# Another order of issue for ScalarE, VectorE, GpSimd and SyncE in a decoder-layer kernel with a fixed order of matmuls

## The chip, the core and the metric

The kernel runs on one core of a Trainium2 chip. A core has five engines that are met below under the profile's names: PE (TensorE, the matmuls; PEld is its load of the stationary operand), DVE (VectorE), ACT (ScalarE), POOL (GpSimd) and SP (SyncE, which here only issues DMAs). Each engine runs its own list of instructions strictly in order; engines wait for each other on semaphores. The metric is the device time of one execution in microseconds (us); the median over several executions is compared.

## The reference

One layer of a decoder trunk for a sequence of 256 tokens, model width 1024, all in float32:

```python
h = RMSNorm(x)
u = h @ W_in            # columns: rnn_x | rnn_gate | q | k | v | branch gates ga, gb
A = GeLU(rnn_gate) * RG_LRU(causal_dwconv4(rnn_x))       # recurrent branch
B = MoBA attention(q, k, v), 8 heads of 128, QK-norm     # one block: causal softmax here
y = sigmoid(ga) * (A @ P_A) + sigmoid(gb) * (B @ P_B)
x = x + y @ W_out
h = RMSNorm(x)
x = x + (GeLU(causal_dwconv3(h @ W_up)) * (h @ W_gate)) @ W_down     # D_FF = 2816
```

RG_LRU is `a = exp(-8 r softplus(-lam))`, then `h_t = a_t h_(t-1) + sqrt(1 - a_t^2) i_t x_t` with r and i two sigmoids of block-diagonal products (8 blocks of 128).

## The kernel before

Every product is taken three times on PE: each float32 operand is split into a rounded high part and the rest, and `hi*hi + hi*lo + lo*hi` is summed in PSUM (`mm3`). Most matmuls have 512 columns; those of attention have 128 or 256.

**Weights stream.** All weights pass in pieces of 1 MB: SP issues the load of `raw` (three buffers), ACT casts it to `hi` (four buffers), DVE subtracts to get `lo` (three buffers), and PE uses both. A piece feeds 24 matmuls. The text numbers the pieces: lo25 is the low half of piece 25. The first four pieces (weights of k) are loaded and split in smaller parts, `raws`, `his`, `los`. In the feed-forward part, quarters of the gate's weights (`wq`) are combined on DVE into sums and differences (`wt`, `wq`) for a seven-product scheme, which PE multiplies as qA, qB and qC.

**Stages of PE, in this order:** k, rx and rg (the recurrent branch's inputs), ri (its two gates), q, ga, v, gb with the scores `s` and the outputs `o` of the eight heads in between, pr (A @ P_A), pa (B @ P_B), wo (W_out), then up, gt and q products, `acc` (W_down), with `last` for the eleventh pair of columns of the feed-forward part and `end` for the last quarter of the output.

**Turns.** Where a result must change between token-major and feature-major, it is not transposed on PE but goes out and in again through DRAM: DVE transposes blocks of 32, SP writes the result in four DMAs and reads it back in one (`turn`, `att_t`, `att_r`). The pairs of names are qd and qm (q), kd and km (k), gr and gm (the recurrent branch's gate), xd and xm, pd and pm (a head's probabilities), md and mm (the merged y), fupd and upm, gq and gtm, fld and lastm. A turned q is split into qTh (ACT) and qTl (DVE), probabilities into pth and ptl, the recurrent branch's result into yah and yal, the attention's into ybh and ybl, the merged y into mh and ml, the feed-forward's into fah and fal, with fla for its last pair.

**Small chains.** The reciprocal roots of the norms are found by three Newton steps on 128x8 values: the tile `rsq`, on DVE to start with and, for q and k, on POOL (`rsqrt(..., pool=True)`); the results for k are `rk`, and k is scaled by them (`kr`) before its turn. ACT's functions lie in tables: an ACT_TABLE_LOAD stands in the list wherever the function next asked for isn't in the table that is loaded. The attention's exponentials (`sm`), the sigmoids of the branch gates (`sga`, `sgb`), tanh, sqrt and gelu share ACT with the casts. The greatest score of each row, with the mask added, is found by DVE (`sm`, `mx`), and POOL holds besides the Newton steps the decay's series (`decw`).

**What sets the order.** The body of the program records operations instead of issuing them: the PE ones in a list of their own, all others in one numbered list. At the end `Later.issue` goes through the string `ORDER`: a number n issues recorded operation n on its engine, `a-b` a run of them, and `+n` the next n matmuls. So `ORDER` sets, for each engine, the order of its list, and nothing else decides it; the order among matmuls is that of their recording. `Pool.buffer` gives a tile the buffer whose last use lies furthest back in the same order. All instructions of the trace have line L247, the call in `Later.issue`; they are told apart by tiles. Semaphores come from the true dependencies. A DMA waits also for the DMA that used its semaphore before it, of which there are eight.

Of the kernel before, what the change touches and what calls it, by code (L numbers as in the profile page):

```python
# [115 lines left out]
+2 39-40 16 +5 41-42 +1 19 18 +1 43 45 47 +2 17 +1 44 46 +4 49-50 48 23 +3 51-52 71 +6 55-56 72 +4 21 53-54 +2 57-58  # L116
+5 22 +4 59-60 +2 63-64 +6 65 61-62 +6 66 +3 67-68 +8 76-77 +4 74 +6 75 +2 93 +1 105-106 +2 73 +3 99 +1 102 +8 108 96
+5 104 +3 78-79 +1 109 +4 80-83 +1 20 69 224 70 +5 107 +2 84-90 +1 91-92 94 +4 142-143 +4 225-226 +4 101 95 +3 110 +5
98 111-112 +3 187-188 141 +5 97 +3 190 117 +1 115 114 116 113 +7 103 +2 227-229 +1 186 118-119 100 120 191 +6 204 +4
121-122 +1 203 +1 123-125 +4 144 126-127 +1 168 145 147 +2 128-129 +5 170 169 146 205 +1 130 230 131 +5 207 +4 171-173  # L120
175 +1 189 174 148-149 132 150 +1 151 133-134 152 +3 135-136 138 +5 137 139-140 +1 153 +3 154-157 +1 177 +1 208 +2 176
199 182 +2 200-201 +2 195-196 +4 158-160 178 +1 197 +2 210 183 +1 198 179-180 +2 202 +1 192 206 +2 212 231-233 +2
234-235 184 181 185 +1 236-238 +1 220 +4 162 211 +2 327 +2 222-223 +5 193 213 219 +1 239-241 +7 161 +1 242-244 +1 221
+4 194 271-272 275 267 +3 276-277 +4 209 245 +2 246-247 282 +4 273 +1 248-251 +1 268-269 274 +1 252-254 +1 278 263 +2
284 +1 285 264-266 +6 295 294 270 279 +2 297 255-257 +4 300 299 258 +1 283 +15 280 +1 281 +3 316 301 +1 298 +1 259 +5
296 +1 260 +1 304 302 +1 261-262 +2 163-164 166 165 167 +4 303 430 332 317 +5 330 +6 315 +4 442 +2 431 +3 333 +1 305
+6 306 331 +3 337 319 +2 320 307-308 362-363 309-310 +2 318 +2 440 322 +6 323 +6 325-326 +3 321 441 +2 329 +1 340 +1
311-312 +3 338 +4 324 +6 365 364 286 366 336 313 +1 214 216 215 217-218 288 314 290 +1 432 367-368 +2 369-371 +2 341
339 +9 360 355 361 +6 433-434 +1 372-377 +3 334 +3 335 +3 356 +1 378 +2 358 +5 328 289 287 +1 443 572 +2 354 291 +3
436 +7 359 +9 392 +1 573 587-588 +1 357 +10 348 344 +2 393 +1 349 352-353 351 350 342 346 343 345 391 292 +2 347 449  # L130
+8 450 452 586 589 451 453-456 +12 435 +4 422-423 538 591 +10 425 402 421 +2 437-438 +1 457-459 +7 460-464 +2 379 +4
380 590 381-382 +2 389 +1 426 +1 465 +10 395 +2 383 394 396 390 +1 424 +2 387-388 384-386 +3 480 484 +2 428 482 +2 404
403 405 +1 439 411-412 +1 481 +6 483 +7 407 398 +4 406 408 410 +1 409 +2 414 +1 413 415 +2 397 416-417 +5 429 +3 489
+1 447 +6 418-420 492 495 494 493 496 506 399-400 +2 445 +2 427 475 507 509 +3 448 401 +5 508 510 444 490 +1 505 +7
466 +1 520 522 467 +3 468 +1 485 491 +4 446 +3 517 521 523 +1 488 476 +1 597 470 469 471 +3 524 +5 293 +1 474 +2 629
487 486 618-619 472-473 533 +2 537 536 535 534 +9 498 +4 497 +1 499 +1 515 478 516 479 +3 477 528 +1 513-514 501 500
# [1206 lines left out]
```

## Time and profile before

| what | before |
|---|---|
| median of 3 runs | 426.13 us (425.86 to 426.56) |
| the profiled execution's own time | 426.22 us |
| its span (first to last instruction) | 424.4 us |
| granted TensorE clock | 1.00 |
| PE busy | 418.9 us, 1908 matmuls |
| DVE busy | 358.2 us |
| ACT busy | 307.4 us, 20.5 of it in 16 table loads |
| POOL busy | 51.0 us |
| DMA | 106.89 MB, mean 252 GB/s |

The timeline view lists instructions with their start in us from the span's start, their duration, engine, line, operation and `out<-in` with shapes; `x2` joins two alike. In brackets stands the idle time of the engine before the instruction, and what ended it. Matmuls are pipelined, so that a 512-column matmul is shown as 0.39 us long while the next one starts 0.227 us after it; the distance from start to start says what one costs, and a longer distance is a wait. The windows view gives the busy time of each engine in a stretch, the granted clock, the share of time in which the DMA engines were busy, and GB/s.

### The profile page before, as it was taken

Reading aid. Unit: us, or ns where it says so; the run is one execution under the profiler, and the core shown is the slowest. Engines: PE = TensorE matmul, PEld = TensorE weight load, DVE = VectorE, ACT = ScalarE, POOL = GpSimd, SP = SyncE. Lnnn points to the kernel's source line nnn. Section 1 sums busy time; section 2 is a strip of 40 time slices with the busy share of each in tenths; the row PEclk is TensorE's granted clock in tenths of the full one; section 3 lists DMA queues with packets and bytes.
Section 4 is the critical chain, followed back from the end, with each engine's and each line's share of the span. In section 5 each row is a group of like instructions: output and inputs, shape, how many; then the busy total and the mean of one; then the engine's idle time right before and its main releaser. Section 6 shows DMA issues by size and latency. Waiting matters only on the chain.

```text
span 424.4 us, 5441 instructions
## 1 busy us (share of the span) xinstructions
PE 418.9 (99%) x1908; PEld 345.9 (81%) x1908; DVE 358.2 (84%) x439; ACT 307.4 (72%) x383; POOL 51.0 (12%) x101
## 2 busy tenths in 40 slices
PE   8999999999999999999999999999999999999997
PEld 7788888888888888878878888888888888888875
DVE  3756979999899999857999765899989798999953
ACT  4767658989889799965434656559885997898630
POOL 1000489707034000000000000000000000000000
PEclk9999999999999999999999999999999999999999
DMA  7986888498997397699896579474597666868702
GB/s 216 415 359 207 261 288 306 131 330 276 298 337 272 100 303 269 224 336 366 259 288 235 174 278 380 176 229 183 155 335 263 201 227 207 260 237 312 281 2 99
DMA packets 46108, 106.89 MB, mean 252 GB/s; under 512 B 8448, under 2 KB 22656, under 8 KB 43648
## 3 DMA queue, kind: packets, MB, share of 16 engines
q1 hardware_dynamic: 45360, 106.01, 73.0%
q10 hardware_dynamic: 720, 0.53, 0.4%
q8 instruction: 15, 0.25, 0.2%
q14 instruction: 13, 0.11, 0.1%
HBM read 92.63 MB, written 13.89 MB: 251 GB/s over the span
## 4 chain that ended last, share of the span: by engine, by line
PE 58%; ACT 18%; DVE 11%; DMA 6%; issue 4%; POOL 2%; SPq 0%; DVEq 0%; ACTq 0%; POOLq 0%
PE acc L247 14%; PE up L247 13%; ACT hi L247 6%; PE qA L247 5%; PE wo L247 5%; PE pa L247 4%; PE k L247 4%; DVE lo L247 4%; PE pr L247 3%; ACT L247 3%; PE qC L247 3%; PE gt L247 3%; PE last L247 3%; DMA pm<-pd 2%; DVE xa L247 2%
## 5 line engine op out<-in xcount | busy, mean ns | idle before, releaser
L247 DVE TENSOR_TENSOR lo<-raw,hi 128x2048 fp32r<-128x2048 f32 (+1 forms) x64 | 141.3, 2214 | 10.8 <-ACT hi L247 10.2
L247 ACT CAST hi<-raw 128x2048 fp32r<-128x2048 f32 (+1 forms) x64 | 118.4, 1856 | 26.0 <-DMA raw<-in_win_fm 6.3
L247 PE MATMUL up<-lo,h2h 128*128 128x512 f32 x80 | 31.1, 389 | 0.0
L247 PE MATMUL up<-hi,h2h 128*128 128x512 f32 x80 | 31.1, 389 | 0.0
L247 PE MATMUL up<-hi,h2l 128*128 128x512 f32 x80 | 31.1, 389 | 0.0
L247 PE MATMUL acc<-hi,fah 128*128 128x512 f32 x78 | 30.4, 390 | 0.0
L247 PE MATMUL acc<-lo,fah 128*128 128x512 f32 x78 | 30.4, 390 | 0.0
L247 PE MATMUL acc<-hi,fal 128*128 128x512 f32 x78 | 30.4, 389 | 0.0
L247 ACT ACT_TABLE_LOAD x16 | 20.5, 1283 | 1.4 <-PEq L1333 1.2
L247 POOL TENSOR_TENSOR rsq<-rsq 128x8 f32<-128x8 f32 x32 | 14.3, 448 | 34.0 <-DVE rsq L247 31.9
L247 ACT CAST hiq<-wq 128x1024 fp32r<-128x1024 f32 x12 | 12.3, 1049 | 8.2 <-PE acc L247 3.0
L247 ACT CAST hit<-wq 128x1024 fp32r<-128x1024 f32 x12 | 12.3, 1050 | 7.9 <-PE up L247 4.4
L247 PEld LDWEIGHTS up<-hi,h2h 128*128 128x128 f32 x80 | 15.0, 188 | 3.2
L247 PEld LDWEIGHTS up<-lo,h2h 128*128 128x128 f32 x80 | 15.0, 188 | 3.1
L247 PEld LDWEIGHTS up<-hi,h2l 128*128 128x128 f32 x80 | 15.0, 188 | 3.1
L247 PEld LDWEIGHTS acc<-hi,fah 128*128 128x128 f32 x78 | 14.6, 188 | 3.1
L247 PEld LDWEIGHTS acc<-lo,fah 128*128 128x128 f32 x78 | 14.6, 188 | 3.1
L247 PEld LDWEIGHTS acc<-hi,fal 128*128 128x128 f32 x78 | 14.6, 188 | 3.1
L247 ACT ACTIVATE fu<-fupd,pv 128x256 f32<-128x256 f32 x32 | 14.8, 506 | 3.0 <-DMA fupd<-upm 2.4
L247 DVE TENSOR_TENSOR loq<-wq,hiq 128x1024 fp32r<-128x1024 f32 x12 | 14.6, 1216 | 1.1 <-PE up L247 1.1
L247 DVE TENSOR_TENSOR lot<-wq,hit 128x1024 fp32r<-128x1024 f32 x12 | 14.3, 1220 | 0.5 <-PE qC L247 0.5
L247 DVE TENSOR_TENSOR wq<-wq,wq 128x1024 f32<-128x1024 f32 x12 | 14.5, 1220 | 0.1
(302 smaller groups left out, 1179.3 us busy)
## 6 DMA issues: line engine op xcount, KB each, us to landing
raw<-in_win_fm SPq DMA_DIRECT2D x16, 1024.0 KB, 7.1
raw<-in_wdown SPq DMA_DIRECT2D x11, 1024.0 KB, 6.1
raw<-in_wup SPq DMA_DIRECT2D x10, 1024.0 KB, 6.3
raw<-in_win_tm SPq DMA_DIRECT2D x8, 1024.0 KB, 7.4
wq<-in_wgate SPq DMA_DIRECT2D x16, 512.0 KB, 7.9
raw<-in_wpr SPq DMA_DIRECT2D x4, 1024.0 KB, 6.2
raw<-in_wpa SPq DMA_DIRECT2D x4, 1024.0 KB, 6.3
raw<-in_wout SPq DMA_DIRECT2D x8, 512.0 KB, 6.2
```

The source lines that it names most:

```text
L247: getattr(engine, name)(*map(real, a), **{n: real(v) for n, v in k.items()})
```

## The change

The string `ORDER` is another one. The instructions are the same but for ACT's table loads, which follow from the order: 16 before, 14 after. PE's list is the same, instruction by instruction. The lists of SP, ACT, DVE and POOL differ from the first instructions on to those of the last pair of the feed-forward part. The string has four lines fewer, so that the call is L243 afterwards. Its first lines:

```diff
 ORDER = """
-26 0-1 4 27-28 3 30 32 2 29 31 +2 5-6 +1 24 +1 25 7 +1 8 +1 9 +1 10 +2 11-12 +2 13 +3 33-34 15 +3 35-36 +2 14 +2 37-38
...
+26 0 24 2 4 1 29 +1 31 3 30 32 +1 5 33 +1 6 35 +1 7 37 +1 8 39 +1 9 +3 10-13 +5 15 34 +3 36 +2 14 +4 16 +2 38 +1 40 +2
...
```

In words, in order of time: SP loads the first column block of x ahead of the first weights, DVE splits that block ahead of the first weights' low half, and the second x loads come earlier; the sums of squares for the first norm and for k are done earlier on ACT and DVE, and the turn of x's second half on DVE stands ahead of lo10; q's first turn stands earlier on DVE and SP; sga's second half gets its sigmoid next to the first half's, in the middle of the gb stage; and of the feed-forward part, sums for the seven products, taps of the convolution and transposes change places by a few positions.

Three places, as the lists have them. First SP while PE is in ri and ga: qm and qd are the writes and the read of q's first turn, km and kd those of k's second one, gm the writes of the gate's turn; the raws are pieces 20, 21, 22, and the list before is:

```order
L247 DMA kd_840<-km_842 128x1024
L247 DMA raw_955<-in_win_tm 128x2048
L247 DMA qm_961<-qd_918 32x4x256 x2
L247 DMA raw_985<-in_win_tm 128x2048
L247 DMA qm_961<-qd_918 32x4x256
L247 DMA gm_991<-gr_989 32x4x256 x4
L247 DMA gm_996<-gr_982 32x4x256
L247 DMA qm_961<-qd_918 32x4x256
L247 DMA gm_996<-gr_982 32x4x256
L247 DMA raw_1013<-in_win_fm 128x2x1024
L247 DMA qd_918<-qm_961 128x1024
```

And after:

```order
L243 DMA qm_895<-qd_887 32x4x256 x4
L243 DMA kd_840<-km_842 128x1024
L243 DMA raw_962<-in_win_tm 128x2048
L243 DMA qd_887<-qm_895 128x1024
L243 DMA raw_996<-in_win_tm 128x2048
L243 DMA gm_999<-gr_991 32x4x256 x2
L243 DMA gm_1002<-gr_993 32x4x256
L243 DMA gm_999<-gr_991 32x4x256 x2
L243 DMA gm_1002<-gr_993 32x4x256 x2
L243 DMA raw_1076<-in_win_fm 128x2x1024
```

The four writes of q stand together and ahead of piece 20, and q's read stands ahead of piece 21 instead of behind piece 22; one of the gate's writes just ahead of piece 22 now has the semaphore that q's read used before it.

Second DVE a little later, at the end of the q stage and the start of v. Before (the `lo` is lo22, `it` the scan of the recurrent branch, `sq` the sums for q's norm):

```order
L247 STREAM_TRANSPOSE qd_1126<-q_1056 128x4x4x32
L247 TENSOR_TENSOR lo_1132<-raw_1013,hi_1107 128x2048
L247 STREAM_TRANSPOSE qd_1126<-q_1062 128x4x4x32
L247 TENSOR_TENSOR qTl_1145<-qd_918,qTh_1141 128x1024
L247 TENSOR_REDUCE sq_1147<-sqq_1128 128x4
L247 TENSOR_REDUCE sq_1147<-sqq_1143 128x4
```

And after:

```order
L243 STREAM_TRANSPOSE qd_1126<-q_1057 128x4x4x32
L243 STREAM_TRANSPOSE qd_1126<-q_1065 128x4x4x32
L243 TENSOR_REDUCE sq_1139<-sqq_1137 128x4
L243 TENSOR_TENSOR qTl_1144<-qd_887,qTh_1135 128x1024
L243 TENSOR_TENSOR lo_1146<-raw_1076,hi_1142 128x2048
```

The low half of q's turn is now ahead of lo22, with one of the two reductions ahead of it.

Third DVE in the pr stage. Before (the `lo` are lo32 and lo33, the `ptl` those of heads 5, 6 and 7):

```order
L247 TENSOR_TENSOR ptl_1787<-pd_1592,pth_1715 128x384
L247 TENSOR_TENSOR lo_1789<-raw_1631,hi_1742 128x2048
L247 TENSOR_TENSOR yal_1791<-it_910,yah_1713 128x1024
L247 TENSOR_TENSOR ybl_1812<-o_1793,ybh_1802 128x4x2x32
L247 TENSOR_TENSOR lo_1841<-raw_1673,hi_1796 128x2048
L247 TENSOR_TENSOR ptl_1843<-pd_1718,pth_1815 128x384
L247 TENSOR_TENSOR ptl_1856<-pd_1757,pth_1854 128x384
```

And after, from behind head 5's `ptl`, which stands six rows earlier here:

```order
L243 TENSOR_TENSOR lo_1792<-raw_1633,hi_1740 128x2048
L243 TENSOR_TENSOR yal_1794<-it_914,yah_1783 128x1024
L243 TENSOR_TENSOR ptl_1803<-pd_1710,pth_1788 128x384
L243 TENSOR_TENSOR ybl_1811<-o_1796,ybh_1805 128x4x2x32
L243 TENSOR_TENSOR lo_1843<-raw_1678,hi_1807 128x2048
L243 TENSOR_TENSOR ptl_1851<-pd_1760,pth_1849 128x384
```

Head 6's `ptl` is now directly behind yal, ahead of a `ybl` and of lo33. In the same way, some 40 us later, the difference `wq_1968<-wq_1968,wq_1916` that stood between lo39 and ml now stands ahead of lo38, and the sum `wt_2093`, which stood there, ahead of a `loq` about 10 us earlier.

More of the change, by code (lines that the diff above doesn't have):

```diff
@@ L120 @@
[L120 to L124, printed above, removed]
@@ new lines @@
+227-230 25 +3 117 100 112 114 118 120 115 113 116 +1 103 144 119 121 +4 122-126 +4 204 +5 191 145 147 +1 203 +2 127 +5
+128-129 +1 146 148 130-131 +1 169 +3 170-171 168 174 205 +1 207 149 132-134 231 150 +4 177 176 199 +6 173 189 +4
+151-158 +1 135-136 175 172 +3 232 +2 139-140 +2 233 +2 234 159-160 235 +1 208 +1 138 137 +3 192 +5 195 +1 200-202 +1
+206 182 +1 196-197 +2 183 +1 236-240 +1 178-179 198 180-181 184-185 162 +3 210 212 +3 220 213 +5 327 +2 241-243 +3 161
+211 +6 219 244-251 +7 222-223 +3 221 +1 193-194 267 271-272 268-269 275-277 +9 263-265 209 +1 252-254 +3 278 273-274
@@ new lines @@
+270 +3 266 +1 255-256 +4 282-283 285 284 257-258 +6 295 279 +2 297 +4 299-300 +6 301 +6 304 +4 280 +1 281 +3 302 316
+294 332 +1 298 +1 259 +5 296 +3 260-261 +2 163 165 164 167 166 +4 317 333 303 262 430 +5 330 +6 315 +4 442 +2 431 +4
+309 305 +3 310 313-314 311-312 +6 319 337 +2 320 440 307 331 306 308 362-364 366 +2 318 +2 322 +6 321 323 +6 325 340
+326 +5 329 +1 360 441 +1 338 432 365 367 +7 324 +6 433 214 286 328 336 +1 218 215 290 217 216 289 288 +1 368-370 +2
+371-374 +11 355 341 361 +6 434 +1 375-378 +3 334 +3 335 +3 436 356 443 +3 358 +5 339 287 +1 572 +2 354 291 +10 359 +10
@@ new lines @@
+573 588 587 +1 357 +10 344 348 +3 349 351 353 342 346-347 352 392 343 393 350 589 345 391 292 +2 586 449-450 452 +8
+451 453-462 +12 435 437 +4 422-423 538 590-591 +10 438 425 402 421 +10 463-465 +2 380 +4 379 381-382 +2 387 389 +1 426
++11 439 +2 383 394 388 390 395-396 428 398 411 +1 424 +2 384 386 385 480 484 481-482 +3 483 +4 404 403 405-407 +1 412
++18 408-410 +4 413-415 +2 416 397 417 +5 429 +3 489 +1 447 +5 444 +1 418-420 492-494 496 495 506 485 399 401 400 520
++2 445 +2 427 475 523 509 507-508 510 +3 448 +6 505 +7 467 466 468 +5 490-491 +4 446 +3 517 522 521 +1 488 476 487 +1
@@ new lines @@
+597 470 469 +3 524 +5 293 +1 474 +2 629 471 473 472 486 618 533 535-536 534 537 +11 498 +5 497 499 +1 515-516 478-479
+619 +3 528 477 +1 617 511-514 501 500 518-519 502 504 598 +6 503 559 +14 529-530 526 +1 539 +6 560 563 +2 561-562 +3
+547 +1 527 +11 540 531-532 +1 542 +1 525 +4 574 +3 544 +3 548 +2 545 581 +4 550 549 551-553 +8 546 +16 564-566 +1 541
+543 +1 554 556 555 575 577 576 578-579 +3 557-558 568 594 567 +7 582 +5 584 +7 592 +1 595 569 571 +1 580 570 601 605
+602 596 604 603 +13 607 620 +3 599 608 593 585 621 +6 600 609 615 613 655 610 +8 583 +1 790 +15 616 +2 606 611-612 625
@@ new lines @@
++4 622-623 +8 785 729 614 +10 627-628 +12 631 731-732 +1 626 630 +5 730 787 +5 789 788 624 +7 640 634 641 +10 733 +2
+635 +11 632 +1 633 +12 638-639 796 734 +1 644 +10 636 +1 637 +9 646-647 +3 648-650 652 654 651 653 +1 663 +13 645 +7
+797 799 657 +2 786 642 +1 658 664 798 +1 656 670 +1 643 +12 659 +4 662 +7 671 +8 677 +17 660 +1 661 697 +4 667 665-666
+668 +6 678 +3 672-673 +10 674-675 +7 698 669 712 +9 801 +1 960 696 676 +1 679 694 680 684 681 683 682 +12 695 800 +2
+716 +3 713 +11 699 +1 685 711 702 700-701 +11 717 +1 727 +10 715 +6 686-688 +4 703 689 705 690 692 691 750 +1 724 +2
@@ new lines @@
++1 892 +10 868 817-818 890 +1 869-873 +3 929 829 778 +10 927 +10 930 +1 925 +2 819 777 779 782 955 +6 893 +1 874 783
+780-781 928 +2 958 +3 1007 956 +2 954 +15 879-880 1008 883 845 884 +5 962 894 +1 886-888 830 889 959 +4 964 +8 957 +7
+931 +3 932 968 +2 963 1009 +5 965 1010 +12 882 881 832 834 831 885 +5 969 +1 1000 1002 +10 967 966 +1 833 +3 848-849
+855 854 846 851 +1 900 +1 857 852 +7 1001 +12 1011 1003 858 +5 1014-1015 +1 850 847 856 853 1016 859-860 916 1018 +5
+1013 +14 1023 +8 917-918 993 1017 1019 971 970 +5 1027 1025 +12 919 1024 1022 1021 +5 1004 +1 912 +5 1030 902 910
@@ new lines @@
+905-906 904 +2 1026 1028 +9 911 907 901 1032 +1 1031 +10 1012 1029 +1 1020 +4 895 897 +2 898-899 896 +3 933 937 934
+936 909 908 903 913 1034 972 935 +3 1033 914 1039 915 +3 1035 +10 1040 1043 +12 920 +2 976 +7 938 +2 1041-1042 +4 1038
+973 975 974 +1 1053 1044 +7 1036 1078 1076 1037 1054 921-922 +11 1052 +7 939-940 +5 950-951 923 +1 977 +3 1088 +7 1079
+1077 924 +2 1045-1047 1050 1049 1048 +4 1091 947 944 +6 1089 952 945-946 941 948-949 942-943 +8 981 987 +3 1055 +4
+1087 982 1056-1057 985 1092 +4 1051 +6 1058 1060 1059 1061 +1 984 +8 1098 953 1099 +5 1101 1094 1093 1095 979 983 980
@@ L166 @@
+978 988 1090 +10 1097 +5 1080 1096 1102 1081 +15 986 989-991 1062 +1 1103 +1 1084-1085 1082-1083 +8 1086 1100 +4 1109
+1104 +8 1064 +1 1063 1065-1067 +2 1068-1071 +11 1110 1072-1075 992 1105 +15 1106-1108 1112 +2 1113 +48 1111 +6
+1114-1115 +3 1116-1117 +3 1118-1119 +5 1120-1121 +1 1122-1123 +5 1124-1125 +1 1126-1127 +6 1128-1129
 """
```

53 lines of the change are left out of this document (8 added, 45 removed).

## The prediction

> **What bounds the kernel now.** First the page: one engine has no room.
>
> ```profile
> PE 418.9 (99%) x1908; PEld 345.9 (81%) x1908; DVE 358.2 (84%) x439; ACT 307.4 (72%) x383; POOL 51.0 (12%) x101
> ```
>
> PE runs through nearly the whole span, and its list and so its work stay as they are. An order can win only what PE loses to waiting. I looked for that in the timeline of PE alone, from start to start: a 512-column matmul is followed by the next 0.227 us later where nothing is in the way. These are the rows on either side of every longer step that matters, and the first of the k stage:
>
> ```profile
> 5.27 0.73 PE L247 MATMUL k<-his,xgh 128*128 128x512 f32 x2
> ...
> 11.54 0.74 PE L247 MATMUL k<-his,xgh 128*128 128x512 f32 x2
> ...
> 79.85 0.39 PE L247 MATMUL q<-hi,xgh 128*128 128x512 f32 x1
> 80.15 0.50 PE L247 MATMUL q<-lo,xgh 128*128 128x512 f32 x1
> ...
> 119.73 0.27 PE L247 MATMUL s<-kTl,qTh 128*128 128x128 f32 x1
> 120.28 0.33 PE L247 MATMUL s<-kTh,qTl 128*128 128x128 f32 x1 [0.28 <-DVE qTl L247]
> ...
> 141.43 0.39 PE L247 MATMUL v<-hi,xgh 128*128 128x512 f32 x1
> 141.73 0.50 PE L247 MATMUL v<-lo,xgh 128*128 128x512 f32 x1
> ...
> 168.81 0.39 PE L247 MATMUL gb<-hi,xgl 128*128 128x512 f32 x1
> 169.55 0.36 PE L247 MATMUL o<-pth,vh 128*128 128x256 f32 x1 [0.35 <-ACT hi L247]
> ...
> 181.51 0.40 PE L247 MATMUL pr<-lo,yah 128*128 128x512 f32 x1
> 182.02 0.50 PE L247 MATMUL pr<-hi,yal 128*128 128x512 f32 x1
> ...
> 184.43 0.28 PE L247 MATMUL o<-pth,vh 128*128 128x256 f32 x1
> 185.03 0.39 PE L247 MATMUL o<-ptl,vh 128*128 128x256 f32 x1 [0.32 <-DVE ptl L247]
> ...
> 222.04 0.39 PE L247 MATMUL wo<-lo,mh 128*128 128x512 f32 x1
> 222.67 0.50 PE L247 MATMUL wo<-hi,ml 128*128 128x512 f32 x1 [0.24 <-DVE ml L247]
> ...
> 403.94 0.39 PE L247 MATMUL acc<-hi,fal 128*128 128x512 f32 x1
> ```
>
> The bracket shows only part of a wait, since the end of the pipelined matmul before it covers the rest: 222.04 to 222.67 is 0.63, of which 0.40 is waiting. The matmul behind a wait also lasts 0.50 in place of 0.39, another 0.11. So I get, as wait plus that: S1 at 80 us 0.07 + 0.11 = 0.18; S2 at 120 us 0.55 less about 0.11 for a 128-column step = 0.44; S3 at 141 us 0.18; S4 at 169 us 0.74 - 0.23 = 0.51; S5 at 182 us 0.28 + 0.11 = 0.39; S6 at 185 us 0.60 less 0.12 for a 256-column step, + 0.11 = 0.59; S7 at 222 us 0.51. S8, at the end of the feed-forward part, is measured below. The head, 5.27 to 11.54, is 24 matmuls (12 rows of two) of 0.227, or 5.45, in 6.27: 0.82 of waiting. Next, who ends each wait; DVE's timeline, except where said:
>
> ```profile
> 119.04 1.18 DVE L247 TENSOR_TENSOR qTl<-qd,qTh 128x1024 fp32r<-128x1024 f32 x1
> ...
> 139.38 2.29 DVE L247 TENSOR_TENSOR lo<-raw,hi 128x2048 fp32r<-128x2048 f32 x1
> ...
> 169.32 0.09 DVE L247 DVE_READ_ACCUMULATOR2_ANT mx<- 128x1 f32 x1
> ...
> 180.75 1.22 DVE L247 TENSOR_TENSOR yal<-it,yah 128x1024 fp32r<-128x1024 f32 x1
> ...
> 220.26 1.22 DVE L247 TENSOR_TENSOR wq<-wq,wq 128x1024 f32<-128x1024 f32 x1
> 221.40 1.22 DVE L247 TENSOR_TENSOR ml<-md,mh 128x1024 fp32r<-128x1024 f32 x1
> ...
> 404.28 0.69 DVE L247 TENSOR_TENSOR fla<-flu,fla 128x512 fp32r<-128x512 f32 x1 [0.74 <-ACT fla L247]
> ```
>
> Each ends 0.05 to 0.15 us ahead of PE's start behind a wait. At S4 the profile names ACT, whose cast was over long before; the `mx` of head 6 ends at 169.41, and the next matmul writes PSUM that it frees. S1 and S3 wait for a `lo`. In S8 the three steps behind 403.94 would end at 404.62; DVE's fla ends at 404.97 and so holds PE until 405.0, 0.4 late. All waits behind the head add up to 2.80 without S8, 3.2 with it. **This is the most that can be won there**, 0.75% of the whole.
>
> **The change part by part.** I price it against the profiled execution's own 426.22 us (1.8 us more than its span, the launch around it), which is 0.09 above the median of the runs.
>
> *Head.* The first weights are loaded behind x's first block, and split behind it, so the first k matmul may start up to 0.8 later: one more xT load ahead, two DVE pieces changed over. What holds PE at 11.54 is in the chain of waits:
>
> ```profile
> 4.47 6.37 DMA raws<-in_win_tm
> 10.87 0.63 ACT his L247
> ```
>
> Those loads are the same, the same number of bytes lie ahead of them, and the waiting of 0.82 absorbs the later start. Price 0; ends: 0.3 gained (an earlier landing) and 0.7 lost (all of it late).
>
> *S1 and S3* hang on how far DVE is behind. Its worst idle time in the first half is in DVE's rows, and the chain of waits names the cause:
>
> ```profile
> 51.42 2.29 DVE L247 TENSOR_TENSOR lo<-raw,hi 128x2048 fp32r<-128x2048 f32 x1
> ...
> 57.12 1.30 DVE L247 TENSOR_TENSOR kr<-kr,rk 128x512 f32<-128x512 f32 x2 [2.27 <-POOL rk L247]
> ```
>
> ```profile
> 51.40 2.37 POOL rsq L247
> ```
>
> A POOL multiply of no more than 128x8 numbers is on the path for 2.37 us, just as long as lo10 beside it. After the change the sums of squares are ready earlier, fewer foreign POOL operations stand within rk's chain, and xd's transpose stands ahead of lo10. I take DVE to be 2 to 3 us earlier from there, so S1 (0.07 of waiting) goes, and S3, for which lo25 must also make good the 0.62 that S1 and S2 gave back. Price -0.36; ends 0 and -0.36.
>
> The Trainium skill, "SBUF — State Buffer", section "Who interferes with whom", says that a DVE instruction with two SBUF inputs and a GpSimd instruction that reads SBUF exclude each other, the one issued first keeping the shared ports to its end. These rows agree (51.40 + 2.37 = 53.77; 51.42 + 2.29 = 53.71). By that rule the chain would still be caught by lo10, only later in the chain, since lo10 still stands ahead of kr; the sum would then lack S1 and S3 and, through S4, become that of rival 1.
>
> *S2.* qTl, which ended at 120.22, had lo22 ahead of it, 2.2 us; now it has one reduction of 128x512 instead, which I price like fla's 0.69, so it ends about 1.5 earlier, with 0.44 + 0.18 needed. lo22 goes behind it and ends at about 121; its user is at 122.44:
>
> ```profile
> 122.44 0.39 PE L247 MATMUL ga<-lo,xgh 128*128 128x512 f32 x1
> ```
>
> Price -0.44. It rests on q's read landing early enough, and so does raw22 behind it: rival 3.
>
> *S4.* Between 142 and 169 things are shuffled within head 6's masks, lo30, and the pd and pth. PE would come 0.80 earlier (S1 to S3) and the masks must too, or the wait grows. Two table loads less shorten ACT:
>
> ```profile
> L247 ACT ACT_TABLE_LOAD x16 | 20.5, 1283 | 1.4 <-PEq L1333 1.2
> ```
>
> One lies ahead of S4: 1.28 us less there, with a sigmoid moved ahead of head 5's exponentials in exchange. Without a row for the new order I take the masks as much earlier as PE: price 0, ends -0.51 and +0.80.
>
> *S5, S6.* ACT is 2.57 us shorter by here, so hi32 and what DVE does after it (lo32, yal) start earlier; yal ended at 181.97 and must be 0.28 + 0.80 sooner. Head 6's ptl was over only just before 185.03 because lo33 and a ybl were ahead of it. Now it follows yal at once, and its only other gate is its cast:
>
> ```profile
> 182.41 0.51 ACT L247 CAST pth<-pd 128x384 fp32r<-128x384 f32 x1 [2.05 <-DMA pd<-pm]
> ```
>
> Even with the landing unmoved, ptl is over at 183.5, against the 184.55 at which PE asked. Price -0.39 and -0.59; ends 0 for both if ACT's gain doesn't reach DVE.
>
> *S7.* ml no longer has the 1.22 of `wq` between it and lo39. That difference still runs on DVE a little earlier, but the `wt` sum that stood there moves back to about 203 us, into a gap:
>
> ```profile
> 205.01 0.69 DVE L247 TENSOR_TENSOR sgb<-pa,sgb 128x512 f32<-128x512 f32 x1 [0.73 <-PE pa L247]
> ```
>
> 0.73 of its 1.22 is covered, so ml ends 0.73 earlier, at 221.9, and 0.40 was needed. Price -0.51; ends 0 and -0.51.
>
> *Feed-forward part and S8.* Between 223 and 403 PE doesn't wait, and the transposes, sums and taps are moved by no more than one to three places; where a transpose on DVE is put ahead of a `lo`, it fills a gap there. I see no `lo` that gets late, and price it at nothing; DVE's gaps are the cover, and without it a transpose costs its 1.2. S8 ends a chain of short ACT and DVE pieces that starts with the landing of raw65, whose load follows lo62 on SP; one short tap of the convolution leaves DVE's list ahead of that point. I take half of S8: -0.2; ends -0.4 and, if the loads don't come earlier with PE, +2 (rival 2).
>
> Sum: 0 - 0.36 - 0.44 + 0 - 0.39 - 0.59 - 0.51 - 0.2 = -2.5, so 426.22 - 2.5 = **423.7 us**.
>
> **The rivals.** *1: DVE is no earlier up to 169 us.* POOL's chain is caught again, kr waits until 57, and whatever PE gains at 80 to 141 is lost at S4, whose masks stay at 169.4. Against it: S2 rests on an order alone, and more than one step was brought forward. For it: the port rows above. It leaves S5 to S8: 426.22 - 1.69 = 424.5.
>
> *2: the last gate stands still.* The DMA engines are nearly full where raw64, raw65 and the last turns are fetched:
>
> ```profile
> 390.00:400.00 10.00, 10.00 (x46) 8.29 (x45) 9.40 (x9) 6.08 (x7) 0.00 (x0) 1.00 0.95 343
> ```
>
> If those landings are set by bandwidth, fla ends at 405.0 whenever PE comes, and all that was won is waited for there: 426.2, no change. Against it: each of these loads is issued only when DVE frees a buffer, and DVE before that is paced by PE, so they are asked for earlier by as much as PE is.
>
> *3: SP blocks behind q's turn; slower.* Piece 22 is now behind q's read and a gate's write that waits for that read's semaphore. Rows of SP, of the page's DMA and cost lists and of the view by tile for qd (all its DMAs):
>
> ```profile
> 95.29 0.92 SPq L247 DMA_DIRECT2D qm<-qd  x2
> ...
> 107.93 0.34 SPq L247 DMA_DIRECT2D qd<-qm  x1
> ```
>
> ```profile
> raw<-in_win_fm SPq DMA_DIRECT2D x16, 1024.0 KB, 7.1
> ```
>
> ```profile
> L247 ACT CAST hi<-raw 128x2048 fp32r<-128x2048 f32 (+1 forms) x64 | 118.4, 1856 | 26.0 <-DMA raw<-in_win_fm 6.3
> ```
>
> ```profile
> DMA to landing us min/median/max: 3.0/5.7/7.9
> ```
>
> raw22 needs 7.1 to land, a cast of 1.9 and a lo of 2.3 before 122.44, so it decides from an issue at 111.1. q's two transposes move ahead of lo17, 2.3 us, so the writes begin near 93.0 and are all issued by 95; with 5.7 to 7.9 for the writes and again for the read, it lands between 106 and 111: just in time. Should it land as late as a read from 107.93 does, 113.6 to 115.8, PE waits 2.5 to 4.7 at 122; S5 to S7 then give back 1.5 at most: 427.2 to 429.4, say 428.
>
> That the change doesn't do what it says is not among them: the lists show the moves.
>
> **How the numbers follow.** Forecast 0.55 (its own range 422.9 to 424.4: all of S4 and S8 gone, or S1, S3 and S8 kept); rival 1 0.15, rival 2 0.18, rival 3 0.12. A measurement can tell about 0.2%, 0.85 us, from no change. Faster by more: forecast and rival 1, less 0.02 = 0.68; the same: rival 2 and that rest = 0.20; slower 0.12. The range leaves out rival 3 and the outer half of the forecast's edge: low is 426.22 - 3.2 - 0.3 (head) = 422.7, with 0.2 of spread between runs 422.5; high is rival 2 with the same spread, 426.4.
>
> **What would show it.** PE's rows at 80, 120, 141, 182, 185 and 222 us come in even steps of 0.227; DVE's kr has no wait for POOL; the read of qd lands before 111; 14 table loads; fla's end moves from 405.0 to about 402.7. It is wrong if kr still waits to 57, if PE waits at the first ga matmuls, or if the wait at fla is longer than 0.4.

## The result, and the profile after

| | before | after |
|---|---|---|
| median of the runs | 426.13 us (5 runs, 425.86 to 427.09) | 424.16 us (5 runs, 423.66 to 424.38) |
| ratio, 95% interval | | 0.9947 [0.9932, 0.9961] |
| the profiled execution, its span | 426.22, 424.4 us | 424.38, 422.6 us |

The changed kernel is faster by 0.53%; the prediction said 423.7 us, 422.5 to 426.4. First the page of the changed kernel, for PE and for the table loads (busy us, share of the span, instructions; then a row of the costliest groups):

```profile
PE 416.9 (99%) x1908; PEld 345.8 (82%) x1908; DVE 359.5 (85%) x439; ACT 304.8 (72%) x381; POOL 51.4 (12%) x101
...
L243 ACT ACT_TABLE_LOAD x14 | 18.0, 1283 | 1.4 <-PEq L1329 1.2
```

PE has the same 1908 matmuls in 2.0 us less. Where they were lost before is told by PE's timeline of the changed kernel, in the pairs of rows that answer to the pairs shown in the prediction; a pair 0.227 us apart (0.12 for 256 columns, 0.11 here for the scores of 128) holds no wait:

```profile
11.11 0.40 PE L243 MATMUL k<-los,xgh 128*128 128x512 f32 x1
11.95 0.74 PE L243 MATMUL k<-his,xgh 128*128 128x512 f32 x2 [0.44 <-ACT his L243]
...
80.30 0.39 PE L243 MATMUL q<-hi,xgh 128*128 128x512 f32 x1
80.53 0.39 PE L243 MATMUL q<-lo,xgh 128*128 128x512 f32 x1
...
119.98 0.28 PE L243 MATMUL s<-kTl,qTh 128*128 128x128 f32 x1
120.09 0.28 PE L243 MATMUL s<-kTh,qTl 128*128 128x128 f32 x1
...
141.20 0.39 PE L243 MATMUL v<-hi,xgh 128*128 128x512 f32 x1
141.43 0.39 PE L243 MATMUL v<-lo,xgh 128*128 128x512 f32 x1
...
168.52 0.39 PE L243 MATMUL gb<-hi,xgl 128*128 128x512 f32 x1
169.35 0.36 PE L243 MATMUL o<-pth,vh 128*128 128x256 f32 x1 [0.44 <-DVE mx L243]
...
181.29 0.39 PE L243 MATMUL pr<-lo,yah 128*128 128x512 f32 x1
181.52 0.40 PE L243 MATMUL pr<-hi,yal 128*128 128x512 f32 x1
...
183.82 0.28 PE L243 MATMUL o<-pth,vh 128*128 128x256 f32 x1
183.94 0.28 PE L243 MATMUL o<-ptl,vh 128*128 128x256 f32 x1
...
220.85 0.39 PE L243 MATMUL wo<-lo,mh 128*128 128x512 f32 x1
221.08 0.39 PE L243 MATMUL wo<-hi,ml 128*128 128x512 f32 x1
...
402.24 0.39 PE L243 MATMUL acc<-hi,fal 128*128 128x512 f32 x1
402.46 0.46 PE L243 MATMUL acc<-hi,fla 128*128 128x512 f32 x1
402.76 0.39 PE L243 MATMUL acc<-lo,fla 128*128 128x512 f32 x1
403.15 0.74 PE L243 MATMUL acc<-hi,fla 128*128 128x512 f32 x2
```

Six of the eight waits are gone: S1, S2, S3, S5, S6 and S7 come in even steps. S4 is there still and a little longer, 169.35 - 168.52 - 0.227 = 0.60 in place of 0.51, and this time the profile names DVE's `mx` as its end. At S8 0.23 is left (403.15 against the even 402.92) of 0.41. The head took 0.41 longer in this execution: the k stage waits until 11.95, not 11.54. A second profile of the changed kernel, after_again below, agrees behind the k stage but for S7: the step before ml is 0.33 there (220.39 to 220.72) and the next 0.33 too, so 0.2 of the 0.51 is left. DVE's timeline of the changed kernel shows who is early now; the `lo` in it is lo30, and behind it stand head 6's masks:

```profile
54.46 1.30 DVE L243 TENSOR_TENSOR kr<-kr,rk 128x512 f32<-128x512 f32 x2
...
116.80 1.22 DVE L243 TENSOR_TENSOR qTl<-qd,qTh 128x1024 fp32r<-128x1024 f32 x1
...
166.36 2.29 DVE L243 TENSOR_TENSOR lo<-raw,hi 128x2048 fp32r<-128x2048 f32 x1
...
169.12 0.08 DVE L243 DVE_READ_ACCUMULATOR2_ANT mx<- 128x1 f32 x1
...
178.89 1.21 DVE L243 TENSOR_TENSOR yal<-it,yah 128x1024 fp32r<-128x1024 f32 x1
...
181.38 0.56 DVE L243 TENSOR_TENSOR ptl<-pd,pth 128x384 fp32r<-128x384 f32 x1 [1.27 <-ACT pth L243]
...
219.38 1.23 DVE L243 TENSOR_TENSOR ml<-md,mh 128x1024 fp32r<-128x1024 f32 x1 [0.23 <-ACT mh L243]
...
402.40 0.69 DVE L243 TENSOR_TENSOR fla<-flu,fla 128x512 fp32r<-128x512 f32 x1 [0.74 <-ACT fla L243]
```

kr has no wait for POOL and starts 2.66 us earlier. What became of POOL's chain is in these rows, POOL's and DVE's, two from before and then four from after (`xd` is the transpose that was put ahead of lo10, and the `lo` behind it is lo10):

```profile
48.89 2.10 POOL L247 TENSOR_TENSOR rsq<-rsq 128x8 f32<-128x8 f32 x1 [0.53 <-DVE rsq L247]
...
56.89 0.20 POOL L247 TENSOR_TENSOR rk<-rk,rs 128x8 f32<-128x8 f32 x1
```

```profile
45.03 2.52 POOL L243 TENSOR_TENSOR rsq<-rsq 128x8 f32<-128x8 f32 x2
...
50.63 0.20 POOL L243 TENSOR_TENSOR rk<-rk,rs 128x8 f32<-128x8 f32 x1
...
51.13 1.25 DVE L243 STREAM_TRANSPOSE xd<-xs 128x1024 f32<-128x1024 f32 x1 [3.55 <-ACT xs L243]
52.29 2.25 DVE L243 TENSOR_TENSOR lo<-raw,hi 128x2048 fp32r<-128x2048 f32 x1
```

Before, two multiplies of the chain up to the first rk were as long as a `lo` (at 48.89, and at 51.40 in the prediction's row); after, one is, beside lo9. The chain also begins 3.1 us earlier (its first multiply at 45.03, before at 48.16), so rk is over at 50.83 and not at 57.09. DVE then idles 3.55 us in another place, ahead of xd, for ACT's xs, and kr comes when xd and lo10 are done.

qTl is over at 118.0, two us ahead of PE; yal at 180.10 and ptl at 181.94 are 1.4 and 2.0 ahead; ml, at 220.61, is 0.5 ahead. Only the `mx` at 169.20 is late. fla ends at 403.09 and not at 404.97, so it followed PE by 1.9. Last SP, and the view by tile of qd:

```profile
88.24 1.99 SPq L243 DMA_DIRECT2D qm<-qd  x4
...
93.16 0.32 SPq L243 DMA_DIRECT2D qd<-qm  x1
```

```profile
DMA to landing us min/median/max: 2.7/3.4/6.4
```

q's writes begin at 88.24 and its read is issued at 93.16, so that it lands before 100 (the longest of these DMAs took 6.4).

Set beside the terms of the prediction, in the profiled executions:

| term | predicted | in the profiles |
|---|---|---|
| head | 0 | +0.41 |
| S1, S3 | -0.36 | -0.36 |
| S2 | -0.44 | -0.44 |
| S4 | 0 | +0.09 |
| S5, S6, S7 | -0.39, -0.59, -0.51 | the same |
| S8 | -0.2 | -0.18 |
| sum | -2.5 | -1.97 |

The times of the two executions differ by 426.22 - 424.38 = 1.84; the remaining 0.13 is spread over the span in pieces that I didn't place.

### The profile page after: what moved, and what is told of

Its sections match the earlier page's. It is cut to its first block, busy times and chain, and to the rows that moved or that the text cites. A ratio compares the mean times of both kernels' runs of the same rounds, so it can differ in the third digit from the quotient of the medians.

```text
span 422.6 us, 5428 instructions
## 1 busy us (share of the span) xinstructions
PE 416.9 (99%) x1908; PEld 345.8 (82%) x1908; DVE 359.5 (85%) x439; ACT 304.8 (72%) x381; POOL 51.4 (12%) x101
## 4 chain that ended last, share of the span: by engine, by line
PE 68%; DVE 14%; ACT 11%; issue 3%; DMA 2%; POOL 1%; SPq 1%; DVEq 0%; ACTq 0%
PE acc L243 14%; PE up L243 13%; PE pr L243 5%; PE qA L243 5%; PE wo L243 5%; PE pa L243 5%; PE rx L243 5%; DVE lo L243 5%; PE k L243 4%; ACT hi L243 3%; PE qC L243 3%; PE gt L243 3%; PE last L243 3%; DVE xa L243 2%; ACT L243 2%
## 5 line engine op out<-in xcount | busy, mean ns | idle before, releaser
L243 DVE TENSOR_TENSOR lo<-raw,hi 128x2048 fp32r<-128x2048 f32 (+1 forms) x64 | 141.5, 2215 | 10.1 <-ACT hi L243 7.5
L243 ACT CAST hi<-raw 128x2048 fp32r<-128x2048 f32 (+1 forms) x64 | 118.6, 1857 | 24.7 <-DMA raw<-in_wup 8.1
L243 PE MATMUL up<-lo,h2h 128*128 128x512 f32 x80 | 31.2, 389 | 0.0
L243 PE MATMUL up<-hi,h2h 128*128 128x512 f32 x80 | 31.2, 389 | 0.0
L243 PE MATMUL up<-hi,h2l 128*128 128x512 f32 x80 | 31.1, 389 | 0.0
L243 PE MATMUL acc<-hi,fah 128*128 128x512 f32 x78 | 30.4, 390 | 0.0
L243 PE MATMUL acc<-lo,fah 128*128 128x512 f32 x78 | 30.4, 389 | 0.0
L243 PE MATMUL acc<-hi,fal 128*128 128x512 f32 x78 | 30.4, 389 | 0.0
L243 POOL TENSOR_TENSOR rsq<-rsq 128x8 f32<-128x8 f32 x32 | 21.9, 688 | 37.3 <-DVE rsq L243 35.3
L243 ACT CAST hiq<-wq 128x1024 fp32r<-128x1024 f32 x12 | 12.3, 1048 | 8.2 <-PE up L243 4.0
L243 PEld LDWEIGHTS up<-hi,h2l 128*128 128x128 f32 x80 | 15.0, 188 | 3.1
L243 PEld LDWEIGHTS up<-hi,h2h 128*128 128x128 f32 x80 | 15.0, 188 | 3.1
L243 PEld LDWEIGHTS up<-lo,h2h 128*128 128x128 f32 x80 | 15.0, 188 | 3.1
L243 PEld LDWEIGHTS acc<-hi,fal 128*128 128x128 f32 x78 | 14.6, 188 | 3.1
L243 PEld LDWEIGHTS acc<-hi,fah 128*128 128x128 f32 x78 | 14.6, 188 | 3.1
L243 PEld LDWEIGHTS acc<-lo,fah 128*128 128x128 f32 x78 | 14.6, 188 | 3.1
L243 ACT ACTIVATE fu<-fupd,pv 128x256 f32<-128x256 f32 x32 | 14.8, 504 | 2.6 <-DVE fc L243 2.6
L243 DVE TENSOR_TENSOR loq<-wq,hiq 128x1024 fp32r<-128x1024 f32 x12 | 14.5, 1219 | 2.0 <-PE up L243 1.8
L243 ACT CAST hit<-wq 128x1024 fp32r<-128x1024 f32 x12 | 12.2, 1048 | 5.1 <-PE up L243 5.1
L243 DVE TENSOR_TENSOR wq<-wq,wq 128x1024 f32<-128x1024 f32 x12 | 14.6, 1214 | 0.2
L243 DVE TENSOR_TENSOR lot<-wq,hit 128x1024 fp32r<-128x1024 f32 x12 | 14.1, 1218 | 0.4 <-ACT hit L243 0.4
```

The source lines that it names most:

```text
L243: getattr(engine, name)(*map(real, a), **{n: real(v) for n, v in k.items()})
```

## The experiments

Two theories stood against each other. **Repairs:** the change is a handful of separate repairs, each a few instructions put ahead of one wait, and each worth that wait by itself. **Lead:** it is a lead of DVE and ACT, built up in the first half and kept by an order in which all engines agree, so that a single move out of it pays little. Every kernel below differs from the kernel before or the one after in `ORDER` alone and leaves the computation as it is. The kernel before had medians of 426.46, 426.64 and 426.51 us in the three groups of runs (23, 23 and 17 runs): the first beside b_head, a_oldhead, b_three and a_best, the second beside b_xd1, a_to150, b_to150 and a_table, the third beside b_paired, a_masks and the repetitions of a_best and of the changed kernel. Each ratio is to the kernel before of its own group, and each profile is of one of the executions. A number in `ORDER` is an operation, `+n` the next n matmuls.

**b_head: the kernel before with the new head,** up to the 48th matmul of k.

```diff
-26 0-1 4 27-28 3 30 32 2 29 31 +2 5-6 +1 24 +1 25 7 +1 8 +1 9 +1 10 +2 11-12 +2 13 +3 33-34 15 +3 35-36 +2 14 +2 37-38
+26 0 24 2 4 1 29 +1 31 3 30 32 +1 5 33 +1 6 35 +1 7 37 +1 8 39 +1 9 +3 10-13 +5 15 34 +3 36 +2 14 +4 16 +2 38 +1 40 +2
...
```

> The order of before, but with the changed order up to the 48th matmul of the k stage. Theory (the new head costs what my forecast left out): the first k matmul comes near 5.1, the fifth pair of column blocks waits longer for its weights, and the row that started at 11.54 starts at 11.9 to 12.0; everything behind it as before, each wait 0.4 later, so 426.6 us. Rival (the 0.41 us later start at 11.95 in the profile of the changed kernel is chance in one execution's DMA): that row starts at 11.5 again within 0.15, and the time is 426.1.

426.22 us (12 runs), ratio 0.9999 [0.9988, 1.0011]. The k stage's wait ends at 11.39. The new head costs and gains nothing that can be told.

**a_oldhead: the changed kernel with the old head,** the same lines the other way round.

> The changed order, but with the order of before up to the 48th matmul of the k stage. Theory: the row at 11.95 comes back to 11.54 and the whole kernel with it, unless the next fixed wait takes the 0.4 back: 423.8 us, or 424.2 if the wait at 169 us grows from 0.60 to 1.0. Rival (chance): 11.9 again, 424.2.

423.95 us (5 runs), ratio 0.9945 [0.9932, 0.9958], the wait's end at 11.41. The 0.41 of the profile was one execution's own. In 14 profiled executions that wait ends at 11.18 to 11.95: at 11.60 in the mean of six with the new head, at 11.42 in that of eight with the old one. A cost of 0.2 can't be excluded.

**b_three: the kernel before with three of the repairs alone.** On DVE lo22 (393) stands behind the first qTl, head 6's ptl (600) directly behind yal, and the `wq` difference and `wt` sum (799, 796) ahead of sga and of a `loq`.

```diff
-357 +10 348 344 +2 393 +1 349 352-353 351 350 342 346 343 345 391 292
+357 +10 348 344 +3 349 352-353 351 350 342 346 343 393 345 391 292
...
-+6 610 +1 599 608 655 +1 583 +1 790 606 +15 616 600 +2 625
++7 599 608 655 +1 583 +1 790 606 +15 600 610 616 +2 625
...
-639 734 +1 644
+639 796 734 +1 644
...
-797 657
+797 799 657
...
```

> The order of before with three moves on DVE alone: lo22 behind the low half of q's turn; head 6's ptl directly behind yal, ahead of a ybl and lo33; and the two sums for the seven products out from between lo38, lo39 and ml. Theory (each wait has its own cause on DVE, but what is won ahead of a gate that doesn't move is lost there): the steps at 120, 185 and 222 us become even; the wait at 169 us grows from 0.51 to about 0.95, because head 6's masks stay at 169.4, so that the first move brings nothing; sum -0.59 - 0.51 = -1.1: 425.0 us. Rival (the waits add up independently): the wait at 169 stays 0.51 and the time falls by 1.54 to 424.6. Second rival (the waits only pass on to the next late DVE instruction): less than 0.4 gained.

427.53 us (12 runs), ratio 1.0021 [1.001, 1.0033]: **slower**, by 0.2%. Of the three expectations only the second rival leaves room for that. The waits S2 and S6 are gone, but new ones stand at 137 (0.77) and 191 (0.39); S7 isn't gone but longer (0.69 of waiting ahead of `wo<-hi,ml` in place of 0.40), and S1 and S3 are longer too. ACT's and DVE's timelines of this kernel show the first cause:

```profile
116.64 0.69 ACT L247 ACTIVATE sqq<-q,rs 128x512 f32<-128x512 f32 x1 [1.41 <-DVE qd L247]
...
118.31 1.23 DVE L247 TENSOR_TENSOR qTl<-qd,qTh 128x1024 fp32r<-128x1024 f32 x1 [1.11 <-ACT qTh L247]
```

qTl, put ahead, meets a qTh that isn't done. ACT's list holds `sqq` ahead of qTh, and that `sqq` reads a q in PSUM which DVE's transpose reads first: the program makes the second reader wait on the first. The Trainium skill, "PSUM — Partial Sum Buffer", section "Terms", says that two engines on one bank at once are an error, reads against reads included; no run here lets them meet, and in b_three ACT waits for that, in b_paired below DVE. DVE loses 1.1 there and is late with what follows up to 137. The second cause is on SP. These are its rows, first in b_three, then in the kernel before (the load of piece 36 and, behind it, two of gate quarters):

```profile
186.97 0.37 SPq L247 DMA_DIRECT2D raw<-in_wpa  x1
187.38 1.02 SPq L247 DMA_DIRECT2D wq<-in_wgate  x2
```

```profile
184.56 0.37 SPq L247 DMA_DIRECT2D raw<-in_wpa  x1
184.97 1.02 SPq L247 DMA_DIRECT2D wq<-in_wgate  x2
```

lo33, put behind ptl, frees its buffer 2.4 us later; the load that waits for that buffer holds up SP, and the gate quarters behind it come 2.4 later too. Without what goes with them on ACT and SP, these three moves cost.

**b_paired: b_three with ACT and SP set to match.** `sqq` (344) stands ahead of the transpose (348), and the load of piece 36 (614) behind the gate quarters.

```diff
-357 +10 348 344 +3 349
+357 +10 344 348 +3 349
...
-622-623 +8 614 +2 613
+622-623 +10 613
...
-631 729 731 785 +1 626
+631 729 731 785 614 +1 626
...
```

> The three DVE moves of b_three on the order of before, now with what the changed order has beside two of them: the square sum of q's second half on ACT ahead of the first DVE transpose of that half, so that ACT's qTh no longer stands behind it; and on SP two loads of gate weights ahead of piece 36, whose load waits for the later lo33. Theory (the moves failed alone because qTh and SP's queue weren't moved with them): no DVE wait for qTh before qTl, no wait at 137 us, ptl of heads 6 and 7 and ml in time, so at least 1.1 us better than before, 425.3 us or less where before is 426.5, and over 2 better than b_three's 427.5. Rival (the moves pay only with the lead that the changed order's first part gives DVE): a new wait at 137 or 191 us remains, 426 us or more.

425.61 us (12 runs), ratio 0.9976 [0.9961, 0.999]: 1.9 us less than b_three, and between the two expectations. DVE's rows of qTl and of ml have no wait now:

```profile
117.65 1.18 DVE L247 TENSOR_TENSOR qTl<-qd,qTh 128x1024 fp32r<-128x1024 f32 x1
...
220.26 1.22 DVE L247 TENSOR_TENSOR ml<-md,mh 128x1024 fp32r<-128x1024 f32 x1
```

S2, S6 and S7 are gone, 0.14 is left at 137 and 0.29 near 190. So both causes named for b_three bear out, each by its own sign (qTl without a wait, and no wait for ml), and the repairs pay 0.9 us once the other engines' lists agree with them. Both were set right in one kernel, so what each is worth alone isn't shown.

**b_xd1: the kernel before with xd's second transpose (171) ahead of lo10 (205),** in one execution.

```diff
-170 169 146 205 +1 130 230 131 +5 207 +4 171-173
+170 169 146 +1 130 230 131 +5 207 +4 171 205 172-173
...
```

> The order of before with one exchange on DVE: the turn of x's second half ahead of lo10. Theory 1 (only the multiply that lo10 blocked is freed): POOL's chain, 2.2 us shorter, ends near 55, kr starts there in place of 57.1, and the wait at 80 us goes. Theory 2 (POOL's next operation is caught by lo10 in turn, as the skill's port rule has it): another POOL multiply of the chain lasts about 2 us beside lo10, kr starts within 0.5 of 57.1, and the wait at 80 us stays at 0.1 to 0.4.

426.47 us. POOL's and DVE's timelines of this kernel:

```profile
52.23 2.88 POOL L247 TENSOR_TENSOR rsq<-rsq 128x8 f32<-128x8 f32 x3
...
52.24 2.25 DVE L247 TENSOR_TENSOR lo<-raw,hi 128x2048 fp32r<-128x2048 f32 x1
...
56.76 1.30 DVE L247 TENSOR_TENSOR kr<-kr,rk 128x512 f32<-128x512 f32 x2 [2.27 <-POOL rk L247]
```

lo10 comes 0.8 later, catches POOL's chain one link later, and kr waits for the same 2.27. The Trainium skill's rule ("SBUF — State Buffer", section "Who interferes with whom") has DVE's instruction and POOL's exclude each other, and the row of 2.88 beside the one of 2.25 agrees. That the one issued first keeps the ports isn't shown: POOL's row starts 0.01 ahead, and it is POOL that is held. Of the move of xd I had expected a part of DVE's lead; alone it gives none.

**a_to150 and b_to150: one half of the change each,** cut at the 600th matmul, 148 us: a_to150 follows the new order up to there and the old one behind it, b_to150 the other way round. The cut in the changed kernel's string, for a_to150:

```diff
-429 +3 489 +1 447 +5 444 +1 418-420 492-494 496 495 506 485 399 401 400 520
+429 +3 489 +1 447 +6 418-420 492 495 494 493 496 506 399-400
...
```

> The changed order up to matmul 600 (near 148 us), the order of before from there. Theory (the parts add up, since head 6's masks follow PE at some steps' distance): the waits at 80, 120 and 141 us stay away, the wait at 169 stays 0.5 to 0.6, and those at 182, 185, 222 and 404 us are as before: -0.80, or 425.5 us where before is 426.3. Rival 1 of the prediction (what is won up to 141 is lost at 169, whose masks come no earlier): the wait at 169 grows to 1.3, and the time is 426.3.

424.87 us (12 runs), ratio 0.996 [0.9948, 0.9971]: 1.8 us less than before, more than twice the waits S1 to S3, and less time than either expectation. They are gone, **and S4 is gone too**; DVE's and PE's timelines (`lo` is lo30):

```profile
164.49 2.29 DVE L245 TENSOR_TENSOR lo<-raw,hi 128x2048 fp32r<-128x2048 f32 x1 [0.44 <-ACT hi L245]
...
167.72 0.08 DVE L245 DVE_READ_ACCUMULATOR2_ANT mx<- 128x1 f32 x1
...
167.95 0.36 PE L245 MATMUL o<-pth,vh 128*128 128x256 f32 x1
```

lo30 starts 1.9 earlier than in the changed kernel, and the masks are done in time. Of the 1.9, PE's rows ahead of this wait account for 0.8 (167.71 here, 168.52 there), so against PE lo30 is 1.1 earlier. S1 to S4 are 1.3; the other 0.5 I didn't place. A part of it may be S2: it is 0.44 in the profile of the kernel before, but 0.70 in b_head's and b_xd1's and 1.04 in b_to150's, whose order there is that of before. So it is the second half of the new order that keeps S4. S5 is 0.62 here in place of 0.39; S6 to S8 stand about as before.

> The order of before up to matmul 600 (near 148 us), the changed order from there. Theory: the waits at 80, 120 and 141 us as before, those at 182, 185 and 222 us gone, that at fla half gone: -1.49 - 0.2 or 424.6 us where before is 426.3. Rival (the second part needs the lead of DVE and ACT that the first part gave): some of the waits at 182 to 222 us come back, over 425.2 us.

425.63 us (12 runs), ratio 0.9977 [0.9968, 0.9987]: 1.0 us. The time is the rival's, the sign isn't: S5 to S7 are gone, S2 is 1.04 in its profile and a new wait of 0.57 stands at 164. The halves give 1.77 and 1.01; in sum 2.8, where the whole gives 2.0 to 2.5.

**a_table: the changed kernel with sga's second sigmoid (617) back behind its old neighbour,** so that there are 16 table loads again.

```diff
-477 +1 617 511-514 501 500 518-519 502 504 598 +6 503 559 +14 529-530 526 +1 539
+477 +1 511-514 501 500 518-519 502 504 598 +6 503 559 +14 529-530 526 617 +1 539
...
```

> The changed order, with the sigmoid of sga's second half behind the cast of hi29 again, as before the change, so that ACT loads 16 tables and not 14. Theory (2.57 us of ACT are what made hi32, yal and the ptl early): yal, which had 1.1 us to spare at 181 us, is late by over 0.5, and the masks of head 6 come no earlier: 424.8 us or more where the changed kernel is 424.2. Rival (ACT waits for data around there, 4.7 us ahead of head 6's pth, so the loads fall into that gap): no new wait at 181 or 185 us, 424.2 us.

424.78 us (6 runs), ratio 0.9957 [0.9942, 0.9972]: 0.4 to 0.8 us of the gain is given back, going by the changed kernel's two ratios, 0.9947 and 0.9938, whose intervals overlap with this one. It isn't lost where I had booked it. DVE's and PE's timelines (of the slowest of the six, 425.61 us):

```profile
166.20 0.56 DVE L243 TENSOR_TENSOR ptl<-pd,pth 128x384 fp32r<-128x384 f32 x1 [1.37 <-ACT pth L243]
...
169.66 0.36 PE L243 MATMUL o<-pth,vh 128*128 128x256 f32 x1 [1.17 <-ACT hi L243]
...
191.12 0.40 PE L243 MATMUL o<-ptl,vh 128*128 128x256 f32 x1 [0.21 <-DVE ptl L243]
```

ACT is late with a pth, DVE waits 1.37 for it with lo30 and the masks queued behind, S4 grows to 1.33, and a wait appears at 190. At S5 and S6 nothing waits: yal ends 1.45 later, at 181.55, and is still in time.

**a_masks: the changed kernel with head 6's masks (551) ahead of lo30 (548).**

```diff
-544 +3 548 +2 545 581 +4 550 549 551-553
+544 +5 545 581 +4 550 549 551 548 552-553
...
```

> The changed order with one exchange: head 6's masks on DVE ahead of lo30. Theory: the wait at 169 us (0.68 with its slow first matmul) is that of the masks alone and goes, nothing else gets late: 423.5 us where the changed kernel is 424.2. Rival (another gate stands right behind): a wait of over 0.3 between 169 and 222 us, 423.9 or more.

423.78 us (6 runs), ratio 0.9934 [0.992, 0.9948]. S4 is gone; in the profiled execution, the slowest of the six (424.46), a wait of 0.47 stands at 190 instead, where head 7's ptl comes late; ACT waits 1.55 there for the pd that is cast ahead of it, 0.85 in the changed kernel. In a_best below, with the same order there, this wait doesn't stand in either profile, so the move isn't shown to cause it.

**a_best: a_masks with the old head, and lo65 behind fla;** run in two groups, in the second beside the changed kernel itself.

```diff
-1110 1072-1075 992 1105
+1072-1075 1110 992 1105
...
```

> The changed order with three further changes: the order of before up to the 48th matmul, head 6's masks on DVE ahead of lo30 in place of behind it, and lo65 behind the last pair's products in place of ahead of them. Theory: the wait at 169 us (0.60 + 0.08) goes, the head gives 0.41, and of the 0.3 at fla at least half goes: 424.16 less 0.41, 0.68 and 0.2, or 422.9 us, unless yal at 181 us or ml at 220 us, which had 1.1 and 0.4 us to spare, become late. Rival (the order is so tight that something else gets late for each thing won): 423.8 or more.

> The kernel a_best again, beside the changed kernel on the same chip. Theory (it has no wait behind the k stage, and its spread is that of the loads ahead of it): 422.8 to 423.6 us, at least 0.5 below the changed kernel in the same call. Rival (its lead makes it late for loads in part of the executions, so that the time is no better): within 0.3 of the changed kernel.

> The changed kernel once more, unedited, on the same chip as the runs below. Theory (the later start of the row at 11.95 was one execution's DMA): that row starts between 11.3 and 11.7, and the waits behind it are those of the first profile, 0.6 at 169 us and 0.3 at fla; 424.2 us. Rival (the new head costs 0.4): 11.9 to 12.0.

a_best gave 423.52 us (422.59 to 424.53) and then 423.29 us (423.00 to 423.64), ratios to before 0.993 [0.9914, 0.9947] and 0.9921 [0.9907, 0.9936]. The changed kernel beside the second gave 424.06 us (423.83 to 424.26), ratio 0.9938 [0.9925, 0.9951]. Six runs each, and their ranges don't meet: this order beats both kernels, by 0.77 us the changed one. The 422.9 us of the first expectation was 0.6 too low; the second, 422.8 to 423.6, holds. In both of its profiles the waits view names no wait of PE behind the k stage.

## Why the prediction was right, and where its steps were not

The time came out 0.5 above the forecast and within the range. In the last group of runs the same two kernels are 2.45 us apart (426.51 and 424.06), nearly the forecast's 2.5; what groups differ by is as much as the miss. Point by point:

- **What can be won.** That PE's list is fixed and only its waits can go held: six of the waits named went, 2.29 us, and with S4, S8 and the head as measured they make 1.97, where the two profiled executions differ by 1.84.
- **The head, 0.** Right as far as the runs can tell: b_head and after_again, which have the new head too, end the wait at 11.39 and 11.52 and have none of the 0.41 of the first profile. In the mean of all profiles the new head's wait ends 0.18 later, which is less than single executions differ by.
- **S1, S3 and DVE's lead.** The size was right and "2 to 3 us earlier" measured 2.66, but of the three grounds one fell: xd's transpose ahead of lo10 gives nothing (b_xd1). What is left are the earlier sums of squares, by which the chain begins 3.1 us earlier and meets one `lo` less, and fewer foreign POOL operations (each 0.2 us); this is read from the profiles, and I haven't run those alone. The prediction feared that lo10 would catch the chain later on; it does catch a multiply at 52.43 (2.18 us), but one behind the first rk, for which this kr doesn't wait. DVE now idles for ACT's xs instead, ahead of xd.
- **S2, -0.44.** The wait went, and the size fits the one profile of before from which it was read; that is luck, since S2 was 0.70 to 1.04 in the three other profiles with that order (b_head, b_xd1, b_to150). The reason, one `lo` less ahead of qTl, is only half of it. Without ACT's `sqq` moved too, qTl waits 1.11 for qTh (b_three, b_paired).
- **S4, 0.** Mis-sized in the direction that the bounds allowed. I took "the masks as much earlier as PE". The lead from the first half would have removed the wait whole (a_to150: 1.8 in place of the 0.8 of S1 to S3), and the second half takes it back, with lo30 later: 0.60. a_masks shows that the masks put ahead of lo30 are in time. But lo30 stands ahead of them in the kernel before and in a_to150 too, so the order of these two alone isn't the cause; it takes a later DVE as well. In the changed kernel DVE waits 0.78 for ACT's pth at 160.51, and a table load stands ahead of the exponentials before that pth, from 157.60 on; in a_to150 the same ptl runs at 159.17 without a wait. I haven't run that by itself, and in a_table, where the load starts 1.2 earlier, a later pth is late instead. What I lacked was to price the two halves apart.
- **S5, S6.** Sizes right, ground wrong: "ACT is 2.57 us shorter by here" is true, but a_table puts the loads back and neither wait returns. In b_to150 both go without the lead of the first half, so it is the second half's order that ends them; which of its moves frees yal isn't shown. What the loads are worth (0.4 to 0.8 us, not clear of the noise) shows at S4 and at 190.
- **S7, -0.51.** Right in the first profile, where ml ends 0.5 ahead of PE although it waited 0.23 for ACT's mh; in after_again 0.2 of S7 is left, so the margin is thin.
- **S8, -0.2.** Measured -0.18.
- **The rivals.** The first fell, since kr no longer waits and a_to150's masks follow DVE's lead. The second fell, since fla moved 1.9 with PE: the load of raw65 was issued 1.7 earlier (385.46, before 387.19), as I had argued, and landed in 6.9 us, not 8.3. What else it shared the DMA engines with changed too (the four writes of gtm begin at 392.43 and not at 390.33), so the runs don't tell how much bandwidth there decides. The third fell by a wide margin: q's read is issued at 93.16 and lands before 100; I had put its landing at 106 to 111, because I had the writes begin near 93, not 88, and had each DMA take 5.7 to 7.9, where the median is 3.4.

Of the two theories, neither holds whole. The repairs at S2, S6 and S7 are real, since three moves end them, but those moves pay only when the lists of the other engines are changed with them. The lead of the first half is worth about 1.8 us, the second half about 1.0. How much of the lead each of the earlier moves makes stays open.

## What to carry to other kernels

Where one engine has no room and its list is fixed, list its start-to-start steps that are too long: their sum bounds what a new order can win (3.2 us here behind the head, of which a_best won 2.9 to 3.2), and behind each here stood one late instruction. Price a move with the instructions that pass it on other engines and with the DMA that waits for the buffer it frees, since everything behind that DMA on its queue moves too (2.4 us here); b_three lost by both what b_paired won back. And split a large reorder by region before splitting it by wait: two halves told here what no single move could, that one half had already removed a wait which the other put back.

## What the runs showed of the hardware

- A POOL multiply of 128x8 values takes 0.20 us alone, and 2.1 to 2.4 when it meets DVE's `lo` of 128x2048, in every order tried here. Moving lo10 alone only changed which link of the chain was caught (b_xd1: three links in 2.88 at 52.23; before: three in 2.92 at 51.40). The chain that begins earlier meets one `lo` in place of two (the changed kernel: two links in 2.52, beside lo9).
- A table load takes 1.28 us (14 in 18.0), and ACT's next instruction starts 0.01 later in b_three's timeline: 111.07 + 1.28, then 112.36. Two loads fewer made 2.6 us of ACT's time; of the kernel's time they made 0.4 to 0.8 us by a_table, with overlapping intervals.
- From one execution to another the old head waits until 11.18 to 11.70 us (eight executions) and the new one until 11.32 to 11.95 (six), and S2 was 0.44 in the profile of before and 1.04 in b_to150's, with the same order up to there. A single profile prices these waits to no better than that.
